# GpSimd's elementwise work in the long convolution runs on VectorE

## The chip, the cores and the metric

The kernel runs on one core of one Trainium2 chip. The metric is the device time of one execution, in microseconds (us); the median of three runs is 2259.96 (2259.07 to 2260.71). A core has TensorE (PE in the profile, PEld for its weight loads), VectorE (DVE), ScalarE (ACT), GpSimd (POOL) and SyncE (SP), which here issues most of the DMAs. Each engine executes its own queue in order and waits for the others by semaphores.

## The reference

One encoder layer on 512 tokens of width 2048: a projection, a gated mixer on one half of its columns, a Hyena operator on the other, an output projection, a gated feed-forward block, norms between them. The change is in the Hyena operator's convolution:

```python
u = bv * bx1
yc = bidir_long_conv(u, k).astype(x.dtype) + u * hy_d_skip[l]
y_b = bx0 * yc

def bidir_long_conv(v, k):
    L = v.shape[1]
    V = jnp.fft.rfft(v.astype(jnp.float32), n=2 * L, axis=1)
    K = jnp.fft.rfft(k, n=2 * L, axis=0)
    return jnp.fft.irfft(V * K[None], n=2 * L, axis=1)[:, :L]
```

## The kernel before

Matrices are multiplied to full fp32 accuracy as three products of fp32r pairs: `exact_pair` casts a tile to its high part on ScalarE (line 131) and subtracts it on VectorE for the low part (line 132); `mm3` issues high times high, low times high, high times low (lines 170 to 172). Weights stream in units of two K tiles by 512 columns: a DMA into `raw`, a cast `hi`, a difference `lo`, three buffers of each.

The stage of the change multiplies the first half of the output projection (`po`, 12 matmuls of 512 columns to a K tile) and works on the long convolution between its K tiles. The convolution goes in four chunks c = 0 to 3 of 256 channels, each in these steps:

- `turn`: 8 transposes on TensorE (`ut`) and the pair `uH`, `uL`.
- `forward`: 24 matmuls of 256 columns (`fw`), sums of cosines and sines.
- `products`: ScalarE copies two banks, VectorE takes sums and differences (lines 829, 830) and the butterfly (339 to 344) into `G`: two frequency halves i, each with a real and an imaginary part of 512 columns.
- `products2`: the complex product with the filter `kh`. For each half there are four multiplications, two on VectorE (840, 842) and two on GpSimd (841, 843), and then a difference and a sum on VectorE (847, 848).
- `spectra`, parity 0 and then 1: the sum, or the difference, of the halves, the real part on VectorE (856) and the imaginary part on GpSimd (857), and then the pair `sH`, `sL` of 1024 columns.
- `inverse`, parity 0 and 1: 24 matmuls (`iv`) each, which need `sH` first and `sL` for every third one.
- `finish`: for two tiles of 128 channels the skip term (880, 881), the product with x0 on GpSimd (882), the pair `ybH`, `ybL` (885, 886) and the running sum of squares `acc_b` (892 on ScalarE, 893 on GpSimd).

`go_to(n)` says behind how many K tiles of `po` a step is written. For chunk c the order on TensorE is: `fw`, six K tiles of `po` (72 matmuls), `iv` of parity 0, `ut` of the next chunk, one K tile, `iv` of parity 1, one K tile, and the next `fw`. The last chunk has no `ut`; its inverses stand among the first K tiles of the projection's second half (`po<-ybH`). A scheduler that builds the program may move an instruction a few places within a queue. Behind the stage, `mc` sums `acc_b` over the partitions.

Of the kernel before, what the change touches and what calls it, by code (L numbers as in the profile page):

```python
# [15 lines left out]
ALU = mybir.AluOpType  # L16

P = 128
# [12 lines left out]
CC = 256  # L31
# [11 lines left out]
def encoder_kernel(ctx: ExitStack, tc: tile.TileContext, a: dict, out: bass.AP):  # L43
# [16 lines left out]
    def bank(name):  # L60
        """one of the four banks of the streamed products"""
        return psum.tile([P, 512], F32, tag="mm", name=name, bufs=4)

    def sbank(name):
        """one of the four banks of everything that runs between them"""
        return psum.tile([P, 512], F32, tag="sd", name=name, bufs=4)
# [10 lines left out]
    # ---------------------------------------------------------------- the stream of weights  # L77
    # a unit: rows k0*128.. of a weight, nk K tiles by nc_ columns
# [25 lines left out]
    # beside the long convolution half of the low parts are computed on Pool  # L104
# [13 lines left out]
    def load_raw(key):  # L118
        src, k0, nk, c0, n = key
        raw = wp.tile([P, 2, 512], F32, tag="raw", name="raw", bufs=3)  # L120
        rows = src[k0 * P : (k0 + nk) * P, c0 : c0 + n].rearrange("(k p) c -> p k c", p=P)
        if st_["dma"] == 0:
            # the first one in halves, as the products wait for it
            for k in range(nk):
                SP.dma_start(raw[:, k : k + 1, :n], rows[:, k : k + 1, :])
        else:
            SP.dma_start(raw[:, :nk, :n], rows)
        return raw
# [27 lines left out]
    def next_unit(key):  # L156
        """the exact fp32r pair of the next unit; the two after it are already on their way"""
        i = st_["use"]
        assert plan[i][1:] == key[1:] and plan[i][0] is key[0], (i, key)
        split_to(i + 3)  # L160
        dma_to(i + 4)
        st_["use"] += 1
        return split_units.pop(i)
# [10 lines left out]
    # ---------------------------------------------------------------- x and constants  # L174
# [50 lines left out]
    def rsqrt(r, ss, n):  # L225
        """r = (ss / n + eps) ** -0.5"""
        DVE.tensor_scalar(r, ss, 1.0 / n, EPS, ALU.mult, ALU.add)
        POOL.tensor_tensor(r, r, nhalf.broadcast_to(list(r.shape)), ALU.pow)

    def rms_col(acc, n, name):  # L230
        """squares, to be summed over the partitions too -> 1/rms, [token, 1] per tile of tokens"""
        nt = acc.shape[-1] // P
        o = sbank("mc")
        for t in range(nt):
            PE.matmul(o[:, t : t + 1], acc[:, t * P : (t + 1) * P], ones[:, 0:1], start=True, stop=True)
        r = const.tile([P, NT], F32, tag="rc", name=name, bufs=3)
        rsqrt(r[:, :nt], o[:, :nt], n)
        return r

    def row_of(r, name, nt=NT):  # L240
        """[token, 1] columns -> the same row of tokens on all partitions"""
        o = sbank("mr")
        for t in range(nt):
            PE.matmul(o[:, t * P : (t + 1) * P], r[:, t : t + 1].broadcast_to([P, P]), ident, start=True, stop=True)
        row = const.tile([P, L], F32, tag="rb", name=name, bufs=2)
        ACT.copy(row[:, : nt * P], o[:, : nt * P])
        return row
# [23 lines left out]
    # ---------------------------------------------------------------- implicit filter  # L271
# [7 lines left out]
    # the last layer comes out twice, on both halves of the partitions  # L279
# [25 lines left out]
    # features of the lags: rows 0..63 the high parts, 64..127 the low parts  # L305
# [3 lines left out]
    def mlp_out():  # L309
        h = hcur[-1]  # L310
        t = fm.tile([P, L], F32R, name="h3t")
        ACT.copy(t, h)
        ACT.copy(h3[:FO, :], h[:FO, :])
        DVE.tensor_tensor(h3[FO:, :], h[FO:, :], f32(t[FO:, :]), ALU.subtract)
        # the backward half has no tap at lag 0
        DVE.tensor_copy(h0, f32(h3[:, :P]))
        DVE.tensor_scalar(h0[:, 0:1], f32(h0[:, 0:1]), 0.0, None, ALU.mult)
# [5 lines left out]
    def forward_mm(cs, tab, rH, rL):  # L323
        """cos (0) or sin (1) sums of the four token phases [tok, CC] -> banks [128, 2, CC] of phases 0 1, 2 3"""
        Hs, Ls = tab
        res = []
        for half in range(2):
            o = sbank("fw")
            ov = o.rearrange("p (m c) -> p m c", m=2)
            for m in range(2):  # L330
                r = 2 * half + m
                mm3(ov[:, m, :], Hs[:, r, cs, :], Ls[:, r, cs, :], rH[:, r, :], rL[:, r, :], True, True)
            res.append(o)
        return res

    def butterfly(G, U, T):
        """phase sums (U: 0+2, 1+3; T: 0-2, 1-3) [P, cs, 2, CC] -> frequencies f + 256 j:
        G[:, i, cs, m] holds j = 2 i + m"""
# [13 lines left out]
    def filter_pieces(tab):  # L352
# [31 lines left out]
        for c in range(NCC):  # L384
# [36 lines left out]
            # the sum of both directions goes with cos and their difference with sin;  # L421
            # the odd phases, which the frequencies f + 256 and f + 768 turn by a quarter, need both
# [47 lines left out]
    # ---------------------------------------------------------------- projections  # L470
    def projA(src, c0, nf, done, rhs=None):
        """[feature, token] tiles of h @ src[:, c0 : c0 + nf*128]; done(ps) takes them out of the banks"""
# [33 lines left out]
    # value branch, [token, feature]  # L506
# [22 lines left out]
    ug, x0 = [], []  # L529

    def eo(ap):
        """[P, 512] stored by token modulo 4, seen in token order"""
        return ap.rearrange("p (r m) -> p m r", r=4)
# [4 lines left out]
    # centred depthwise convolutions over tokens (free axis)  # L538
    def conv3(pl, ps, r, names, fb, to=None):
        """to: where the result goes, by token modulo 4; without it, in token order in a passing tile"""  # L540
# [48 lines left out]
    def go_to(n):  # L589
        """emit the products up to K tile n of the projections"""  # L590
        while pos[0] < n:
            next(main)
            pos[0] += 1

    # a_u, with the rest of x and the filter behind its K tiles
# [56 lines left out]
    # spatial gating weights, transposed: [j, h, i]  # L652
# [111 lines left out]
    # ---------------------------------------------------------------- long conv and output projection  # L764
# [42 lines left out]
    def turn(c):  # L807
        """[channel, token] -> [token, channel] pair of u"""
# [25 lines left out]
    def products2(c):  # L834
        (G, U, T), kh = conv[c].pop("G"), conv[c]["kh"]
        for i in range(2):
            vr, vi = flat(G[:, i, 0]), flat(G[:, i, 1])
            kr, ki = kh[:, i, 0, :], kh[:, i, 1, :]
            p1, p2 = flat(U[:, i]), flat(T[:, i])
            DVE.tensor_tensor(p1, vr, kr, ALU.mult)  # L840
            POOL.tensor_tensor(p2, vi, ki, ALU.mult)
            DVE.tensor_tensor(vr, vr, ki, ALU.mult)
            POOL.tensor_tensor(vi, vi, kr, ALU.mult)
        for i in range(2):
            vr, vi = flat(G[:, i, 0]), flat(G[:, i, 1])
            p1, p2 = flat(U[:, i]), flat(T[:, i])
            DVE.tensor_tensor(p1, p1, p2, ALU.subtract)
            DVE.tensor_tensor(vr, vr, vi, ALU.add)
        conv[c]["Y"] = (G, U, T)

    def spectra(c, par):
# [5 lines left out]
        POOL.tensor_tensor(flat(S[:, 1]), i0, i1, op)  # L857
# [17 lines left out]
    def finish(c):  # L875
        Dt, St = quad("T"), quad("U")
        for i in range(2):
# [4 lines left out]
            POOL.tensor_tensor(du, du, x0[ct], ALU.mult)  # L882
# [5 lines left out]
            if ct == 0:  # L888
                ACT.activation(pairs(acc_b), eo(du), AF.Square)
            else:  # L890
                sq = flat(St[:, i])
                ACT.activation(pairs(sq), eo(du), AF.Square)
                POOL.tensor_tensor(acc_b, acc_b, sq, ALU.add)
# [99 lines left out]
    # ---------------------------------------------------------------- ConvGLU  # L993
# [76 lines left out]
    # ---------------------------------------------------------------- the last group, and the final norm  # L1070
    # token halves, so that the first half leaves while the second is computed
# [36 lines left out]
    def rms3():  # L1108
        """1/rms per token from tiles of squares"""
# [17 lines left out]
    for th in range(2):  # L1127
        hs = slice(th * HW, (th + 1) * HW)
        # sums of squares: two running ones; at the end the last tiles go to the tensor engine as they are
# [42 lines left out]
def shape_constants():  # L1172
    """Tables that depend on the sequence length and widths alone."""
# [12 lines left out]
    # transforms of 1024 points at frequencies f + 1/2: forward [m, r, cos/sin, f] for token 4 m + r,  # L1186
    # inverse [f, parity e, cos/sin, kt, (q m)] for frequency f + 256 kt and token 4 m + 2 q + e
# [11 lines left out]
# the vectors that are used as per-partition columns, in one array  # L1199
# [20 lines left out]
def laid_out(inputs, zT):  # L1220
    """The inputs as the kernel reads them: the same numbers, some of them transposed or packed."""
# [31 lines left out]
```

## Time and profile before

| | |
|---|---|
| median of three runs | 2259.96 us (2259.07 to 2260.71) |
| span of the profiled execution | 2257.4 us |
| its own time beside the span | not printed; the runs' median is 2.6 us above the span |
| TensorE busy | 2189.7 us, 97% of the span |
| VectorE busy | 1133.1 us, 50% |
| ScalarE busy | 671.9 us, 30% |
| GpSimd busy | 317.5 us, 14% |
| the stage of the change | about 533 to 709 us of the span |

Busy shares are averages over the whole span. What ends a wait in the stage is read from the waits of TensorE and from the timeline.

### The profile page before, as it was taken

Reading aid. Unit: us, or ns where it says so; the run is one execution under the profiler, and the core shown is the slowest. Engines: PE = TensorE matmul, PEld = TensorE weight load, DVE = VectorE, ACT = ScalarE, POOL = GpSimd, SP = SyncE. Lnnn points to the kernel's source line nnn. Section 1 sums busy time; section 2 is a strip of 40 time slices with the busy share of each in tenths; the row PEclk is TensorE's granted clock in tenths of the full one; section 3 lists DMA queues with packets and bytes.
Section 4 is the critical chain, followed back from the end, with each engine's and each line's share of the span. In section 5 each row is a group of like instructions: output and inputs, shape, how many; then the busy total and the mean of one; then the engine's idle time right before and its main releaser. Section 6 shows DMA issues by size and latency. Waiting matters only on the chain.

```text
span 2257.4 us, 23811 instructions
## 1 busy us (share of the span) xinstructions
PE 2189.7 (97%) x9742; PEld 1782.5 (79%) x9742; DVE 1133.1 (50%) x1320; ACT 671.9 (30%) x851; POOL 317.5 (14%) x201
## 2 busy tenths in 40 slices
PE   7999999999888999999999999999999999999997
PEld 5778887778777888787887878878787887878877
DVE  8664465556676853534336353443534335343456
ACT  5333432222343332222122221222222122221333
POOL 5221121001344520101001010000101001010003
PEclk9999999999898999999999999999999999999998
DMA  6333223243212423222322323222222222222332
GB/s 208 99 109 122 85 87 92 83 131 111 86 66 93 140 93 96 93 92 94 102 95 93 94 92 95 91 96 94 94 92 95 93 94 93 93 94 85 95 120 75
DMA packets 113480, 223.10 MB, mean 99 GB/s; under 512 B 7035, under 2 KB 18491, under 8 KB 111580
## 3 DMA queue, kind: packets, MB, share of 16 engines
q1 hardware_dynamic: 109184, 215.69, 29.5%
q10 hardware_dynamic: 4188, 5.90, 0.8%
q8 instruction: 76, 1.25, 0.2%
q14 instruction: 32, 0.26, 0.0%
HBM read 213.18 MB, written 8.39 MB: 98 GB/s over the span
## 4 chain that ended last, share of the span: by engine, by line
PE 84%; DVE 10%; issue 2%; POOL 1%; DMA 1%; ACT 1%; SPq 0%; DVEq 0%; POOLq 0%; ACTq 0%
PE pa L170 19%; PE pa L172 19%; PE pa L171 19%; PE pd L170 5%; PE pd L172 5%; PE pd L171 5%; DVE cv L559 2%; DVE lo L132 1%; PE po L170 1%; PE po L171 1%; PE po L172 1%; PE pv L170 1%; PE pv L171 1%; PE pv L172 1%; DVE ev L546 1%
## 5 line engine op out<-in xcount | busy, mean ns | idle before, releaser
L132 DVE TENSOR_TENSOR lo<-raw,hi 128x1024 fp32r<-128x1024 f32 (+2 forms) x369 | 462.6, 1256 | 899.5 <-ACT hi L131 899.4
L131 ACT CAST hi<-raw 128x1024 fp32r<-128x1024 f32 (+2 forms) x369 | 382.3, 1036 | 1156.1 <-PE pa L171 738.2
L170 PE MATMUL pa<-h2H,hi 128*128 128x512 f32 x1376 | 543.6, 395 | 0.0
L172 PE MATMUL pa<-h2H,lo 128*128 128x512 f32 x1376 | 543.4, 395 | 0.0
L171 PE MATMUL pa<-h2L,hi 128*128 128x512 f32 x1376 | 543.4, 395 | 0.0
L172 PEld LDWEIGHTS pa<-h2H,lo 128*128 128x128 f32 x1376 | 258.4, 188 | 62.5
L170 PEld LDWEIGHTS pa<-h2H,hi 128*128 128x128 f32 x1376 | 258.4, 188 | 62.4
L171 PEld LDWEIGHTS pa<-h2L,hi 128*128 128x128 f32 x1376 | 258.4, 188 | 62.4
L170 PE MATMUL pd<-aH,hi 128*128 128x512 f32 x640 | 249.8, 390 | 14.8 <-DVE xacc L1048 14.8
L172 PE MATMUL pd<-aH,lo 128*128 128x512 f32 x640 | 249.2, 389 | 0.0
L171 PE MATMUL pd<-aL,hi 128*128 128x512 f32 x640 | 249.1, 389 | 0.0
L1011 POOL TENSOR_TENSOR gg<-gg,r 128x512 f32<-128x512 f32 x43 | 73.9, 1723 | 1243.8 <-ACT gg L1010 1243.8
L172 PE MATMUL pa<-hH,lo 128*128 128x512 f32 x512 | 206.2, 403 | 6.0 <-DVE lo L132 6.0
L170 PE MATMUL pa<-hH,hi 128*128 128x512 f32 x512 | 207.5, 405 | 1.2 <-DVE ev L546 1.2
L171 PE MATMUL pa<-hL,hi 128*128 128x512 f32 x512 | 205.8, 402 | 0.0
L170 PEld LDWEIGHTS pd<-aH,hi 128*128 128x128 f32 x640 | 120.1, 188 | 43.6 <-ACT hi L131 17.2
L172 PEld LDWEIGHTS pd<-aH,lo 128*128 128x128 f32 x640 | 120.1, 188 | 25.1
L171 PEld LDWEIGHTS pd<-aL,hi 128*128 128x128 f32 x640 | 120.1, 188 | 24.9
L1048 DVE TENSOR_TENSOR xacc<-xacc,pd 128x512 f32<-128x512 f32 x160 | 106.0, 685 | 42.4 <-PE pd L172 42.4
L172 PEld LDWEIGHTS pa<-hH,lo 128*128 128x128 f32 x512 | 98.7, 193 | 32.7 <-DVE lo L132 8.1
L170 PEld LDWEIGHTS pa<-hH,hi 128*128 128x128 f32 x512 | 99.0, 193 | 29.1 <-DVE ev L546 4.2
L171 PEld LDWEIGHTS pa<-hL,hi 128*128 128x128 f32 x512 | 98.6, 193 | 22.0
(243 smaller groups left out, 2305.1 us busy)
## 6 DMA issues: line engine op xcount, KB each, us to landing
raw<-in_ffn_w_up SPq DMA_DIRECT2D x160, 512.0 KB, 3.5
raw<-in_ffn_w_down SPq DMA_DIRECT2D x84, 512.0 KB, 3.5
raw<-in_w_in SPq DMA_DIRECT2D x79, 512.0 KB, 3.6
raw<-in_w_out SPq DMA_DIRECT2D x32, 512.0 KB, 3.5
raw<-in_ffn_w_up SPq DMA_DIRECT2D x16, 384.0 KB, 3.2
khat_d<-kh SPq DMA_DIRECT2D x4, 1024.0 KB, 3.9
kh<-khat_d SPq DMA_DIRECT2D x4, 1024.0 KB, 4.8
res<-in_xT SPq DMA_DIRECT2D x4, 1024.0 KB, 4.7
```

Source lines behind the costliest of these rows:

```text
L131: ACT.copy(hi, src)
L132: eng.tensor_tensor(lo, src, f32(hi), ALU.subtract)
L170: PE.matmul(o, ah, bh, start=start, stop=False)
L171: PE.matmul(o, ah, bl, start=False, stop=False)
L172: PE.matmul(o, al, bh, start=False, stop=stop)
L546: DVE.tensor_tensor(eo(e), pairs(o), pairs(r), ALU.mult)
L559: DVE.scalar_tensor_tensor(dd, e[:, from_ : from_ + z_ - a_], w(f), dd, ALU.mult, ALU.add)
L1011: POOL.tensor_tensor(g_, g_, r2[0], ALU.mult)
L1048: DVE.tensor_tensor(x_, x_, o, ALU.add)
```

## The change

Everything that GpSimd did in `products2`, `spectra` and `finish` is issued on VectorE. In `products2` each operation covers both frequency halves in one instruction of 2 x 512 columns. Comments and docstrings are gone too, so the lines behind have other numbers: line 857 of before is 855, 882 is 880, 886 is 884, 893 is 891.

```diff
     def products2(c):
         (G, U, T), kh = conv[c].pop("G"), conv[c]["kh"]
-        for i in range(2):
-            vr, vi = flat(G[:, i, 0]), flat(G[:, i, 1])
-            kr, ki = kh[:, i, 0, :], kh[:, i, 1, :]
-            p1, p2 = flat(U[:, i]), flat(T[:, i])
-            DVE.tensor_tensor(p1, vr, kr, ALU.mult)
-            POOL.tensor_tensor(p2, vi, ki, ALU.mult)
-            DVE.tensor_tensor(vr, vr, ki, ALU.mult)
-            POOL.tensor_tensor(vi, vi, kr, ALU.mult)
-        for i in range(2):
-            vr, vi = flat(G[:, i, 0]), flat(G[:, i, 1])
-            p1, p2 = flat(U[:, i]), flat(T[:, i])
-            DVE.tensor_tensor(p1, p1, p2, ALU.subtract)
-            DVE.tensor_tensor(vr, vr, vi, ALU.add)
+
+        Gv = G.rearrange("p i s m c -> p i s (m c)")
+        vr, vi = Gv[:, :, 0], Gv[:, :, 1]
+        kr, ki = kh[:, :, 0, :], kh[:, :, 1, :]
+        p1, p2 = (t.rearrange("p i m c -> p i (m c)") for t in (U, T))
+        DVE.tensor_tensor(p1, vr, kr, ALU.mult)
+        DVE.tensor_tensor(p2, vi, ki, ALU.mult)
+        DVE.tensor_tensor(vr, vr, ki, ALU.mult)
+        DVE.tensor_tensor(vi, vi, kr, ALU.mult)
+        DVE.tensor_tensor(p1, p1, p2, ALU.subtract)
+        DVE.tensor_tensor(vr, vr, vi, ALU.add)
         conv[c]["Y"] = (G, U, T)
...
         DVE.tensor_tensor(flat(S[:, 0]), r0, r1_, op)
-        POOL.tensor_tensor(flat(S[:, 1]), i0, i1, op)
+        DVE.tensor_tensor(flat(S[:, 1]), i0, i1, op)
...
-            POOL.tensor_tensor(du, du, x0[ct], ALU.mult)
+            DVE.tensor_tensor(du, du, x0[ct], ALU.mult)
...
-                POOL.tensor_tensor(acc_b, acc_b, sq, ALU.add)
+                DVE.tensor_tensor(acc_b, acc_b, sq, ALU.add)
```

First place: VectorE's queue of a chunk from the end of the butterfly to `sL` of parity 0. Before:

```order
L840 TENSOR_TENSOR U<-G,kh 128x512 x2
L842 TENSOR_TENSOR G<-G,kh 128x512 x2
L847 TENSOR_TENSOR U<-U,T 128x512
L848 TENSOR_TENSOR G<-G 128x512
L847 TENSOR_TENSOR U<-U,T 128x512
L848 TENSOR_TENSOR G<-G 128x512
L132 TENSOR_TENSOR lo<-raw,hi 128x1024
L856 TENSOR_TENSOR T<-U 128x512
L856 TENSOR_TENSOR U<-U 128x512
L132 TENSOR_TENSOR lo<-raw,hi 128x1024
L132 TENSOR_TENSOR sL<-T,sH 128x1024
```

The same stretch of the changed kernel:

```order
L841 TENSOR_TENSOR U<-G,kh 128x1024
L842 TENSOR_TENSOR T<-G,kh 128x1024
L843 TENSOR_TENSOR G<-G,kh 128x2x512
L844 TENSOR_TENSOR G<-G,kh 128x2x512
L845 TENSOR_TENSOR U<-U,T 128x1024
L846 TENSOR_TENSOR G<-G 128x2x512
L132 TENSOR_TENSOR lo<-raw,hi 128x1024
L854 TENSOR_TENSOR T<-U 128x512
L855 TENSOR_TENSOR T<-G 128x512
L132 TENSOR_TENSOR lo<-raw,hi 128x1024
L854 TENSOR_TENSOR U<-U 128x512
L132 TENSOR_TENSOR sL<-T,sH 128x1024
```

Eight instructions of 512 columns became six of 1024, the imaginary sum (855) stands among them, and the real difference of parity 1 (854, into U) now comes behind the second `lo`.

Second place: VectorE's queue in the `finish` of chunk 1, up to the first sum of chunk 2 (829); x is the tile x0. Of the changed kernel:

```order
L879 SCALAR_TENSOR_TENSOR T<-iv,rl_111,T 128x512
L880 TENSOR_TENSOR T<-T,x_3539 128x512
L879 SCALAR_TENSOR_TENSOR T<-iv,rl_111,T 128x512
L884 SCALAR_TENSOR_TENSOR ybL<-T,cols,ybH 128x512
L891 TENSOR_TENSOR acc_b<-acc_b,U 128x512
L880 TENSOR_TENSOR T<-T,x_3545 128x512
L132 TENSOR_TENSOR lo<-raw,hi 128x1024
L884 SCALAR_TENSOR_TENSOR ybL<-T,cols,ybH 128x512
L891 TENSOR_TENSOR acc_b<-acc_b,U 128x512
L829 TENSOR_TENSOR U<-fw,G 128x512
```

Before there stood 881 twice, 886 twice, `lo` and 829. The products with x0 (880) and the sums (891) now stand between them; in the `finish` of chunk 0 the one sum comes behind both 884 and the `lo` behind that.

Third place: TensorE's queue where the inverse of chunk 1 begins, as a piece of the difference:

```order
 L170 MATMUL iv<-invH,sH 128x2x128
 L171 MATMUL iv<-invL,sH 128x2x128
+L170 MATMUL iv<-invH,sH 128x2x128
+L171 MATMUL iv<-invL,sH 128x2x128
+L813 MATMUL ut<-ident,u 128x128 x4
 L172 MATMUL iv<-invH,sL 128x2x128
 L170 MATMUL iv<-invH,sH 128x2x128
```

Four matmuls with `sH` and four transposes stand before the first one with `sL` (172), where two matmuls stood. In chunk 0 three matmuls stand there, in chunk 2 four, eight transposes and one of `po`, in chunk 3 four and five of `po`.

## Rows read from the trace of the kernel before

**Rows 1.** The page: the span, and busy time, share and instructions of each engine.

```profile
span 2257.4 us, 23811 instructions
PE 2189.7 (97%) x9742; PEld 1782.5 (79%) x9742; DVE 1133.1 (50%) x1320; ACT 671.9 (30%) x851; POOL 317.5 (14%) x201
```

**Rows 2.** Waits of TensorE: who waited for whom, us in total, times, longest.

```profile
PE iv L170 <- ACT sH L131: 14.4, 4, 4.3
PE iv L172 <- DVE sL L132: 8.9, 4, 2.4
PE mc L235 <- POOL acc_b L893: 1.3, 1, 1.3
```

**Rows 3.** Timeline of TensorE in chunk 0: start, us, instructions [idle before <-releaser].

```profile
545.03 0.28 PE L170 MATMUL fw<-uH,tabH 128*128 128x256 f32 x1
...
566.10 0.39 PE L170 MATMUL iv<-invH,sH 128*128 128x256 f32 x1 [1.66 <-ACT sH L131]
...
569.03 0.39 PE L172 MATMUL iv<-invH,sL 128*128 128x256 f32 x1 [2.43 <-DVE sL L132]
...
573.25 1.05 PE L813 MATMUL ut<-ident,u 128*128 128x128 f32 x8
574.05 0.47 PE L170 MATMUL po<-yh,hi 128*128 128x512 f32 x1
...
579.79 0.40 PE L170 MATMUL po<-yh,hi 128*128 128x512 f32 x1
```

**Rows 4.** The same timeline in chunk 1.

```profile
582.55 0.28 PE L170 MATMUL fw<-uH,tabH 128*128 128x256 f32 x1
...
585.43 0.39 PE L170 MATMUL po<-yh,hi 128*128 128x512 f32 x1
...
606.13 0.58 PE L170 MATMUL iv<-invH,sH 128*128 128x256 f32 x1 [4.17 <-ACT sH L131]
...
609.06 0.58 PE L172 MATMUL iv<-invH,sL 128*128 128x256 f32 x1 [2.14 <-DVE sL L132]
...
620.59 0.40 PE L170 MATMUL po<-yh,hi 128*128 128x512 f32 x1
```

**Rows 5.** TensorE by windows: stretch, its length, busy, PEclk (granted clock), DMA.

```profile
610.00:613.00 3.00, 3.00 (x16) 0.50 0.00 0
```

**Rows 6.** Timeline of VectorE in chunk 1.

```profile
587.61 0.68 DVE L829 TENSOR_TENSOR U<-fw,G 128x512 f32<-128x512 f32 x1
...
592.55 1.28 DVE L840 TENSOR_TENSOR U<-G,kh 128x512 f32<-128x512 f32 x2
...
599.17 1.76 DVE L848 TENSOR_TENSOR G<-G 128x512 f32<-128x512 f32 x1 [1.18 <-POOL G L843]
...
605.59 1.22 DVE L132 TENSOR_TENSOR lo<-raw,hi 128x1024 fp32r<-128x1024 f32 x1
606.72 2.29 DVE L132 TENSOR_TENSOR sL<-T,sH 128x1024 fp32r<-128x1024 f32 x1
```

**Rows 7.** Timelines of GpSimd and of ScalarE in chunk 1.

```profile
597.40 2.99 POOL L843 TENSOR_TENSOR G<-G,kh 128x512 f32<-128x512 f32 x2
...
605.03 1.04 ACT L131 CAST sH<-T 128x1024 fp32r<-128x1024 f32 x1 [7.13 <-DVE T L856]
```

**Rows 8.** Instructions on G: ns min/median/max, first and last start, forms.

```profile
L840 DVE TENSOR_TENSOR U<-G,kh x8: 675/676/686, 552.5 to 674.9; 128x512 f32<-128x512 f32 x8
L841 POOL TENSOR_TENSOR T<-G,kh x8: 1282/2364/3486, 552.7 to 677.9; 128x512 f32<-128x512 f32 x8
```

**Rows 9.** The same view of T, the steps of `finish`.

```profile
L881 DVE SCALAR_TENSOR_TENSOR T<-iv,rl,T x8: 750/751/752, 578.6 to 701.8; 128x512 f32<-128x512 f32 x8
...
L885 ACT ACTIVATE ybH<-T,cols x8: 1214/1236/1237, 580.8 to 704.8; 128x512 fp32r<-128x512 f32 x8
L886 DVE SCALAR_TENSOR_TENSOR ybL<-T,cols,ybH x8: 1144/1158/1162, 582.1 to 706.0; 128x512 fp32r<-128x512 f32 x8
L892 ACT ACTIVATE U<-T x7: 1137/1138/1152, 584.1 to 705.9; 128x512 f32<-128x512 f32 x7
```

## The prediction

> **What bounds the kernel now.** I read the waits of TensorE first, since VectorE and GpSimd are busy for 50% and 14% of the span only [rows 1]. TensorE waits for little: 14.4 us for `sH` and 8.9 us for `sL`, four times each, once per chunk of the convolution, and 1.3 us for `acc_b` [rows 2]. Whatever the change does, it must do there. Next I read TensorE's timeline, to see what such a wait costs. In chunk 0 it idles 1.66 and 2.43 us [rows 3], in chunk 1 4.17 and 2.14 us [rows 4]; taking both from the 23.3 us of the two wait rows leaves 12.9 for chunks 2 and 3, so these are like chunk 1.
>
> The wait is not all of it. An undisturbed chunk, from its first `fw` to the `po` behind the second inverse, takes 2.88 for 24 matmuls of 256 columns, 585.43 to 601.96 (606.13 less the idle 4.17) for 72 of `po`, 16.4 without the last one's tail [rows 4], 2.88 for the first inverse (the shape of `fw`), 0.80 for the transposes [rows 3], a sixth of 16.4 for 12 more of `po`, and 2.88 for the second inverse: 28.6 us. Chunk 0 takes 34.8 [rows 3] and chunk 1 38.0 [rows 4], so they lose 6.2 and 9.4 us, 2.1 and 3.1 more than the idle time. [...] The stage loses 6.2 + 3 x 9.4 = 34.4 us, and 1.3 at `mc`. That is the most that can come back, apart from some clock behind `mc`.
>
> Last I read VectorE and GpSimd in chunk 1, to see why `sH` is late. From the start of 840 at 592.55 to `sH` at 605.03 there are 12.5 us [rows 6, 7]. GpSimd's products take 1.28 us at best but 2.36 in the median and 3.49 at most [rows 8]. The 848 that starts at 599.17 takes 1.76 and ends 0.54 us after GpSimd's last product (597.40 + 2.99 = 600.39) [rows 6, 7], while the shape alone takes 0.68 [rows 8]. So beside each other the two engines take turns, and one pays for the other's operation. The `sL` of 2.29 us beside a `lo` of the same size at 1.22 shows it once more [rows 6]. [...]
>
> **The change part by part.** I count from F, the first `fw` of a chunk. TensorE reaches the inverse at F + 19.3 (601.96 - 582.55, less the tail of a matmul) [rows 4].
>
> *products2.* Six VectorE instructions of 1024 columns replace eight of 512 and four of GpSimd. The nearest row is the low part of 1024 columns, which starts 1.13 us before the next instruction [rows 6]. Six make 6.8 us. The trace has no instruction of this form with two strided halves; I take the contiguous price. Three of the six touch neighbouring parts of G and may wait for the one ahead of them to end, 1.22 instead of 1.13 [rows 6] and some hundredths for the semaphore: 0 to 0.4 us, and I take 0.4, since they rewrite in place what their neighbours read. Chunk 1 begins them at 592.55 = F + 10.0 [rows 6] and ends at F + 17.2.
>
> *spectra, parity 0.* A `lo` (1.13), two sums of 512 (0.6 to the next, 840's two take 1.28 together [rows 6], and 0.68), then the cast of 1.04 [rows 7] and 0.1 for signals: `sH` at F + 20.75, against 606.07 - 582.55 = F + 23.5 now. Behind the sums VectorE does a `lo`, the real difference of parity 1 and then `sL`: 1.13 + 0.6 + 1.22, so `sL` is there at F + 22.5, against F + 26.5 now (609.06).
>
> *finish.* From X, the `po` behind the second inverse (579.79 in chunk 0), the steps alternate between VectorE and ScalarE: 881 ends at 579.3 [rows 9], the product with x0 is there at X + 0.25, `ybH` (1.24) at 1.5, `ybL` (1.16) at 2.7 [rows 9]. The second product with x0 is queued behind this `ybL`, which waits for ScalarE, and ends at 3.3; `ybH` 4.6, the square (1.14) 5.7, the sum (0.68) 6.4. The cast of `hi` is queued behind the square, and `lo` behind that: VectorE starts 829 at X + 7.8, where it starts now (587.61) [rows 6]. So chunk 1 gains nothing here. In the `finish` of chunks 1 and 2 the cast stands ahead of the second `ybH` and `lo` ahead of the second `ybL`, so the last sum ends at X + 7.0: chunks 2 and 3 begin 0.8 us earlier. The two products and one or two sums add 2.0 to 2.7 us to VectorE per chunk; they are hidden in its waits for ScalarE. If that cover were gone, 829 and with it `sH` would move by as much.
>
> *What TensorE then waits.* Chunk 0 has no `finish` ahead of it: 840 starts at 552.5 [rows 8] = F + 7.5 [rows 3], 2.5 us sooner than in chunk 1. `sH` is there at F + 18.25, no wait; `sL` at F + 20.0, three matmuls of 0.12 behind the start at 19.3: wait 0.35. Chunk 1: 1.45 for `sH`; four matmuls and four transposes cover 0.9, then 0.85 for `sL`: 2.3 us. Chunks 2 and 3, 0.8 earlier: 0.65, then a cover of 1.5 to 1.6, then 0.2: 0.85 each. Will the clock still fall? No row has a wait of 2.3 us spread over 3.2; the nearest, chunk 0 of before with 4.1 us, costs 2.1. I take 0 to 2.1 for chunk 1, 1.3 as the value, and 0 for the others.
>
> *mc.* The last sum ends at X + 7.0, and 28 matmuls of `po` (6.4 us) stand ahead of `mc` now: a wait of 0.65 for 1.3.
>
> **The sum.** 34.4 - (0.35 + 2.3 + 1.3 + 0.85 + 0.85) = 28.8, and 0.65 at `mc`: 29.4 us. The queues behind the stage keep their order, so nothing of it is given back. Span 2257.4 [rows 1] - 29.4 = 2228.0; the runs' median lies 2.6 above the span, which gives 2230.6 beside 2259.96 before.
>
> The two ends: every wait and all slow clock gone, with some clock behind `mc`, gives 37 us, 2223. With `sL` and `sH` a further 1.5 us late in each chunk, and the clock falling as in chunk 0, the remains are 1.9, 7, 4.5 and 4.5 us, 18 in all, which gives 2242.
>
> [...] The row has the next instruction start 1.13 us after one of 1.22 [rows 6], which is the price in the sum. [...]
>
> **The rivals.**
> - *The chain stays late.* Strided halves or waits between VectorE's own instructions make the six cost 1.4 us instead of 1.13, and the clock falls in three chunks: the upper end above, 2236 to 2246. For it speaks that the six rewrite G, U and T in place, one behind the other; against it, that two products of 512 that do the same start 0.60 apart now (840's pair takes 1.28) [rows 6]. 17%.
> - *The wait moves.* The stall ends, but VectorE's longer queue delays a `lo` or a `uL` on which `po` or `fw` waits, for some 4 us a chunk: 2246 to 2255. Against it: a `lo` is made two units, four K tiles or 11 us, ahead of its use, and the last one ahead of `iv` moves forward with the chain. 5%.
> - *Slower.* The long durations of 848 are VectorE's own price for these operands and not GpSimd's doing. Then an operation of 1024 columns costs 2 x 1.22, the mean of 1.76 and 0.68 [rows 6, 8], six take 14.6 us, `sH` comes at F + 28.6, 5.1 us later than now, and the stage pays some 18 to 20 us: 2279. It decides from 1.67 us an instruction, where the 3.3 us by which `sH` is early are used up. Against it: 840 reads the same tiles and takes 0.68 in all eight instances [rows 8]. 5%.
> - *No effect.* TensorE meets another wait at the same place, such as the bank of an inverse or the next weights, worth what it saved: 2256 to 2264. No row of TensorE's waits names one. 3%.
>
> **How the numbers follow.** The forecast has 70%, with 2223 to 2236 as its own range. The range 2223 to 2242 adds most of the first rival. A change of 0.2%, 4.5 us, is about what this measurement can tell. Faster: the forecast and the first two rivals, 92%; same 3%; slower 5%.
>
> **What the profile after should show.** TensorE's waits for `sH` and `sL` together at 3 to 7 us instead of 23.3, none for `sH` in chunk 0 and the longest in chunk 1; the six instructions at 1.13 to 1.25 us; no VectorE instruction of this stage above 1.3 us; 829 at X + 7.8 in chunk 1 and X + 7.0 in chunks 2 and 3; a granted clock of 1.0 in chunks 0, 2 and 3. I am wrong if one of the six takes over 1.4 us, if the clock falls in chunks with less than a microsecond of wait, or if a new wait stands under `fw` or `po`.

## The result, and the profile after

The changed kernel takes 2227.07 us in the median of four runs (2226.78 to 2228.73), the kernel before, run beside it, 2259.55 (2259.07 to 2260.71): 0.9857 times, with a 95% interval of 0.9843 to 0.9871. It is faster by 32.5 us. The forecast was 2230.6, in a range of 2223 to 2242.

The page of the changed kernel, the span and the busy time of each engine:

```profile
span 2225.5 us, 23765 instructions
PE 2179.2 (98%) x9742; PEld 1773.4 (80%) x9742; DVE 1134.9 (51%) x1335; ACT 672.4 (30%) x851; POOL 251.8 (11%) x162
```

The first thing to see is VectorE. GpSimd gave up 39 instructions and 65.7 us, VectorE took them all, and its own busy time rose by 1.8 us [rows 1]. By an estimate from the 0.60 to 0.68 us that an operation of 512 columns takes, the 39 would cost VectorE some 24 us. By the same estimate about 22 us of what the profile of before counted as VectorE's work was time in which it stood beside a GpSimd operation.

The waits of TensorE (who for whom, us in total, times, longest), to be held against [rows 2]:

```profile
PE iv L170 <- ACT sH L131: 1.7, 3, 1.0
...
PE iv L172 <- DVE sL L132: 0.6, 1, 0.6
PE mc L235 <- DVE acc_b L891: 0.6, 1, 0.6
```

23.3 us of waits for the spectra became 2.3, and no new one stands under `fw` or `po` in the stage. TensorE's timeline (start, us, instruction, idle time before it), for [rows 3] and [rows 4]:

```profile
545.56 0.28 PE L170 MATMUL fw<-uH,tabH 128*128 128x256 f32 x1
...
574.32 0.40 PE L170 MATMUL po<-yh,hi 128*128 128x512 f32 x1
...
577.08 0.28 PE L170 MATMUL fw<-uH,tabH 128*128 128x256 f32 x1
...
597.45 0.39 PE L170 MATMUL iv<-invH,sH 128*128 128x256 f32 x1 [0.97 <-ACT sH L131]
...
599.25 0.38 PE L172 MATMUL iv<-invH,sL 128*128 128x256 f32 x1 [0.61 <-DVE sL L132]
...
607.80 0.40 PE L170 MATMUL po<-yh,hi 128*128 128x512 f32 x1
...
678.44 1.05 PE L235 MATMUL mc<-ones,acc_b 128*128 128x1 f32 x8 [0.60 <-DVE acc_b L891]
```

Chunk 0, from its first `fw` to the `po` behind its second inverse, takes 574.32 - 545.56 = 28.8 us instead of 34.8, chunk 1 607.80 - 577.08 = 30.7 instead of 38.0; chunks 2 and 3, read in the same way, take 29.5 and 28.5 instead of 38.1 and 37.3. From the last of these `po` to the `mr` behind `mc` it is 12.7 us (671.29 to 684.00) instead of 15.0 (701.58 to 716.58). I call the sum of the five the stage time: 163.3 us before, 130.2 after, 33.1 less. The whole span is 31.9 less; the difference lies outside the stage (its first `fw` alone comes 0.5 us later than in [rows 3]).

TensorE by windows (stretch, length, busy, granted clock, DMA share, GB/s), for [rows 5]:

```profile
597.00:601.00 4.00, 2.94 (x22) 1.00 0.68 226
601.00:605.00 4.00, 4.00 (x25) 1.00 0.42 131
678.00:682.00 4.00, 3.56 (x20) 1.00 0.32 110
```

Before, the granted clock behind the waits was 0.60 in chunk 0 (569.03 to 573.00) and 0.50 in chunk 1 (606.13 to 614.00). By an estimate from TensorE's busy time there, 3.97 us at 0.60 and 5.73 at 0.50, that is 1.6 of the 2.1 us and 2.9 of the 3.1 us that these chunks lost beside their idle time. Now it is 1.00 in chunk 1 in and behind the two waits, and behind `mc` as well. The same view over the whole stage, from the first `fw` to `mr`, before and after:

```profile
545.03:716.58 171.55, 147.04 (x742) 0.89 0.24 83
```

```profile
545.56:684.00 138.44, 135.54 (x742) 1.00 0.31 103
```

VectorE and ScalarE in chunk 1, and the first sum of chunk 2, for [rows 6] and [rows 7]:

```profile
582.15 0.68 DVE L829 TENSOR_TENSOR U<-fw,G 128x512 f32<-128x512 f32 x1
...
587.08 1.22 DVE L841 TENSOR_TENSOR U<-G,kh 128x1024 f32<-128x1024 f32 x1
588.22 1.22 DVE L842 TENSOR_TENSOR T<-G,kh 128x1024 f32<-128x1024 f32 x1
589.35 1.22 DVE L843 TENSOR_TENSOR G<-G,kh 128x1024 f32<-128x1024 f32 x1
...
596.35 1.04 ACT L131 CAST sH<-T 128x1024 fp32r<-128x1024 f32 x1 [3.93 <-DVE T L855]
...
597.97 1.23 DVE L132 TENSOR_TENSOR sL<-T,sH 128x1024 fp32r<-128x1024 f32 x1
...
615.00 0.69 DVE L829 TENSOR_TENSOR U<-fw,G 128x512 f32<-128x512 f32 x1
```

The six take 1.22 us and start 1.13 to 1.14 apart. `sH` ends 10.3 us behind the start of the first (597.39 - 587.08); it was 13.5 behind 840 [rows 6, 7].

### The profile page after: what moved, and what is told of

It reads as the page before. It is cut to its first block, busy times and chain, and to the rows that moved or that the text cites. A ratio compares the mean times of both kernels' runs of the same rounds, so it can differ in the third digit from the quotient of the medians.

```text
span 2225.5 us, 23765 instructions
## 1 busy us (share of the span) xinstructions
PE 2179.2 (98%) x9742; PEld 1773.4 (80%) x9742; DVE 1134.9 (51%) x1335; ACT 672.4 (30%) x851; POOL 251.8 (11%) x162
## 4 chain that ended last, share of the span: by engine, by line
PE 87%; DVE 9%; issue 2%; DMA 1%; ACT 1%; SPq 0%; DVEq 0%; POOL 0%; ACTq 0%
PE pa L170 19%; PE pa L172 19%; PE pa L171 19%; PE pd L170 5%; PE pd L171 5%; PE pd L172 5%; DVE cv L559 2%; PE po L170 2%; PE po L171 2%; PE po L172 2%; PE pv L170 1%; PE pv L171 1%; PE pv L172 1%; DVE lo L132 1%; DVE ev L546 1%
## 5 line engine op out<-in xcount | busy, mean ns | idle before, releaser
L171 PEld LDWEIGHTS pa<-hL,hi 128*128 128x128 f32 x512 | 98.7, 193 | 22.1
```

Of the source, the lines that this page charges most:

```text
L171: PE.matmul(o, ah, bl, start=False, stop=False)
```

## Experiments

**The theories.** A: VectorE and GpSimd take turns, as I read the 1.76 us of 848 beside GpSimd's product for 0.68 without [rows 6, 8], so the way to `sH` and `sL` costs the sum of both, and GpSimd's operations are the dear ones (1.28 us at the least for VectorE's 0.68 [rows 8]); the gain is that they are gone from it. B: the gain comes from fewer and longer instructions, the merging over the halves. C: it comes from `finish`, by an earlier start of the next chunk and the earlier `mc`. The first three kernels are before with one part of the change each; the next five set A and B apart, take `finish` from the other side and look for what is left; the last two are a repeat.

**e1, products2 alone.** Before, with `products2` as in the change; `spectra` and `finish` stay.

```diff
-            DVE.tensor_tensor(p1, vr, kr, ALU.mult)
-            POOL.tensor_tensor(p2, vi, ki, ALU.mult)
...
+        DVE.tensor_tensor(p1, vr, kr, ALU.mult)
+        DVE.tensor_tensor(p2, vi, ki, ALU.mult)
```

> The kernel before with products2 alone as in the change; spectra and finish keep GpSimd. Theory A (VectorE and GpSimd take turns, so the time up to sH and sL is the sum of both, and what the change shortens is this chain): the products bring most, but GpSimd's imaginary sums still take turns with a lo and with sL, so sL comes about 1.4 us later than in the changed kernel; TensorE's waits for sH and sL at 7 to 11 us, 2233 to 2240. Theory B (the larger, fewer instructions are what counts): 2227 to 2230. Theory C (the finish, by which a chunk starts sooner, is what counts): over 2245.

Measured: 2243.09 us, 0.9937 (0.9924 to 0.9951); stage time 146.9, 16.4 less. That is less of a gain than the 2233 to 2240 expected. TensorE's waits:

```profile
PE iv L170 <- ACT sH L131: 10.5, 4, 3.3
...
PE iv L172 <- DVE sL L132: 3.0, 4, 0.8
```

The wait for `sH` is far from gone. Timelines of GpSimd and VectorE where the sums of chunk 1 stand:

```profile
595.31 4.42 POOL L855 TENSOR_TENSOR T<-G 128x512 f32<-128x512 f32 x1 [13.01 <-DVE G L846]
...
597.94 0.68 DVE L854 TENSOR_TENSOR U<-U 128x512 f32<-128x512 f32 x1
600.85 1.23 DVE L132 TENSOR_TENSOR sL<-T,sH 128x1024 fp32r<-128x1024 f32 x1 [2.23 <-ACT sH L131]
```

The one imaginary sum left on GpSimd takes 4.42 us, and the next of the same shape 1.26. It starts at 595.31, while VectorE has work without a gap until 598.62 (597.94 + 0.68), and ends 1.1 us after that. So it did not end behind the next VectorE instruction, as turns would have it, but at 599.73, with three VectorE instructions started in between and the run over, and VectorE then idled 2.23 us for the `sH` made from it. A's direction holds; I had priced the operation by its turns.

**e2, spectra alone.** Before, with `POOL.tensor_tensor(flat(S[:, 1]), i0, i1, op)` on DVE.

> The kernel before with only the imaginary sums of spectra on VectorE. Theory A: sH 0.4 and sL 1.5 us sooner in each chunk, waits for both at 15 to 19 us, 2248 to 2255. Theories B and C: 2258 to 2261, as before.

Measured: 2249.79 us, 0.9957 (0.9944 to 0.9969); stage time 154.1, 9.1 less, as A has it. TensorE's waits, its timeline in chunk 0 and the window behind it:

```profile
PE iv L170 <- ACT sH L131: 12.3, 4, 3.8
...
PE iv L172 <- DVE sL L132: 4.6, 4, 1.3
```

```profile
561.84 0.38 PE L170 MATMUL iv<-invH,sH 128*128 128x256 f32 x1 [1.11 <-ACT sH L131]
...
563.63 0.39 PE L172 MATMUL iv<-invH,sL 128*128 128x256 f32 x1 [1.29 <-DVE sL L132]
```

```profile
565.00:569.00 4.00, 4.00 (x24) 0.61 0.11 42
```

The wait for `sL` halves: the `sL` of parity 0, which took 2.29 us beside GpSimd's second sum, takes 1.21 without it (chunk 1); the wait for `sH`, behind the products, hardly moves. Chunk 0 idles 1.11 + 1.29 = 2.4 us, and the granted clock behind that is low here too (0.61 from 565 to 569). This case is taken up below.

**e3, finish alone.** Before, with the product with x0 and the sum into `acc_b` on DVE.

> The kernel before with only the finish (the product with x0 and the sum acc_b) on VectorE. Theory A: chunks 2 and 3 start 0.8 us sooner, the wait at mc halves and the clock behind it stays up: 3 to 4.5 us, 2255 to 2257. Theory C: half of the gain or more, 2244 or less. Theory B: 2260.

Measured: 2253.02 us, 0.9972 (0.9961 to 0.9982); stage time 155.4, 7.9 less, a little more of a gain than the 2255 to 2257 expected. TensorE's waits:

```profile
PE iv L170 <- ACT sH L131: 13.0, 4, 4.2
...
PE iv L172 <- DVE sL L132: 6.7, 4, 2.4
...
PE mc L235 <- DVE acc_b L893: 0.6, 1, 0.6
```

Of the 7.9, 2.3 are at `mc` (0.7 of wait, the rest the clock behind it: 0.55 from 709.40 to 713.00 before, 1.00 from 703.05 to 706.65 here). The waits for the spectra lose 3.6, all in chunks 2 and 3. These begin 0.7 us earlier, and in chunk 3 TensorE's first matmul with `sL` stands 1.74 us behind the first one with `sH` (684.52 to 686.26), where it stood 2.93 behind (687.93 to 690.86): about the 1.79 of e2's chunk 0 (561.84 to 563.63). C holds for a quarter of the gain and no more. The three parts alone give 16.4 + 9.1 + 7.9 = 33.4 us of stage time and together 33.1. But in each of the three profiles the clock behind `mc` stayed at 1.00, which is worth 1.6 us and can be won once (from the last `po` to `mr` it is 13.4 us in e1 and in e2, with the wait for `acc_b` as before). Counted once, the three give 30.2: nearly the whole, with 3 us that only the parts together bring. TensorE's order can account for these 3 us, by an estimate. In e1 two matmuls, 0.5 us, stand before the first one with `sL`, as before the change. In the changed kernel the scheduler put more work there (the third place in the change): 1.2 us in chunk 1 (597.45 to 599.25 - 0.61) and 1.8 in chunks 2 and 3. With 0.5 us there it would wait some 1.3 us for `sL` in each of the three chunks, 3 us more in all than it does. No run changes that order alone.

**e4, all on VectorE but in halves.** The changed kernel, with the twelve operations of 512 columns in the loops of before, all on DVE. Against the kernel before, `products2` differs in two lines:

```diff
-            POOL.tensor_tensor(p2, vi, ki, ALU.mult)
+            DVE.tensor_tensor(p2, vi, ki, ALU.mult)
...
-            POOL.tensor_tensor(vi, vi, kr, ALU.mult)
+            DVE.tensor_tensor(vi, vi, kr, ALU.mult)
```

> The changed kernel with products2 in two halves again, twelve instructions of 512 columns, all on VectorE. Theory A: twelve at 0.60 make 7.2 us for 6.8, sH 0.4 us later in each chunk: 2228 to 2230. Theory B: most of the gain is lost, over 2240.

Measured: 2225.44 us, 0.985 (0.9836 to 0.9863), below the 2228 to 2230 that A expected; stage time 130.4, that of the changed kernel. In the profiled execution what is lower lies ahead of the stage (see the last section). TensorE's waits:

```profile
PE iv L170 <- ACT sH L131: 2.5, 3, 1.4
...
PE iv L172 <- DVE sL L132: 0.2, 1, 0.2
```

Twelve starts 0.60 us apart take 7.2 us, six 1.13 apart 6.8; the 0.4 show as 0.8 more for `sH` in three chunks, of which 0.4 come back at `sL`.

**e5, merged but shared.** Before, merged over the halves, with p2 and `vi * kr` still on POOL.

```diff
+        DVE.tensor_tensor(p1, vr, kr, ALU.mult)
+        POOL.tensor_tensor(p2, vi, ki, ALU.mult)
+        DVE.tensor_tensor(vr, vr, ki, ALU.mult)
+        POOL.tensor_tensor(vi, vi, kr, ALU.mult)
```

> The kernel before with both halves in one instruction, but shared between VectorE and GpSimd as before. Theory A: GpSimd's two products of 1024 columns take about 2.4 us each and cannot run beside VectorE's, two at 1.13, one sum and one difference at 1.13 make some 9.3 us for 9.5: 2255 to 2262. Theory B: half of the gain or more, under 2245.

Measured: 2256.56 us, 0.9989 (0.998 to 0.9997); stage time 160.1, 3.2 less. Timelines of both engines in chunk 1:

```profile
593.15 3.16 POOL L842 TENSOR_TENSOR T<-G,kh 128x1024 f32<-128x1024 f32 x1 [6.25 <-DVE G L344]
596.40 3.27 POOL L844 TENSOR_TENSOR G<-G,kh 128x1024 f32<-128x1024 f32 x1
...
594.09 3.31 DVE L843 TENSOR_TENSOR G<-G,kh 128x1024 f32<-128x1024 f32 x1
597.32 3.42 DVE L845 TENSOR_TENSOR U<-U,T 128x1024 f32<-128x1024 f32 x1
```

Here it is VectorE that pays. Its instruction that starts while GpSimd's is under way lasts 3.31 us and ends 1.09 behind it (597.40 against 596.31); alone the shape takes 1.22. The next pair repeats it (600.74 against 599.67). With e4 this settles B: merging gives nothing measurable without GpSimd, and a tenth of a per cent with it.

**e6, finish back on GpSimd.** The changed kernel, with the two operations of e3 on POOL again.

> The changed kernel with the finish back on GpSimd. Theory A: chunks 2 and 3 start 0.8 us later, and the wait at mc is 1.3 us again with the clock falling behind it: 2230 to 2233. Theory C: over 2240.

Measured: 2231.48 us, 0.9882 (0.9866 to 0.9897); stage time 135.3, 5.1 more than the changed kernel. TensorE's waits, its timeline in chunk 1, and a window:

```profile
PE iv L172 <- DVE sL L132: 3.5, 3, 1.2
...
PE mc L235 <- POOL acc_b L891: 1.3, 1, 1.3
```

```profile
596.02 0.39 PE L170 MATMUL iv<-invH,sH 128*128 128x256 f32 x1 [1.04 <-ACT sH L131]
...
597.82 0.39 PE L172 MATMUL iv<-invH,sL 128*128 128x256 f32 x1 [1.17 <-DVE sL L132]
```

```profile
599.00:603.00 4.00, 4.00 (x30) 1.00 0.43 147
```

The time is the expected one, but only in part for the expected reason. 0.7 of the 5.1 us are at `mc`, where the wait came back and the clock was still 1.00 behind it (681 to 685); and `sH` comes 0.7 later in chunks 2 and 3, as expected. But 2.9 are more waiting for `sL`, which follows `sH` by 1.8 us as in the changed kernel. What differs is TensorE's order, which the scheduler set anew: three matmuls, 0.6 us (596.02 to 597.82 - 1.17), stand before the first one with `sL`, where the changed kernel has 1.2 to 1.8 us of work. So `finish` itself is worth some 2 us from this side, and the rest is the order. In chunk 1 the clock is 1.00 behind 1.04 + 1.17 = 2.2 us of idle time, in about the pattern of e2's chunk 0, where 0.61 followed 2.4 us.

**e7, GpSimd kept busy beside.** The changed kernel, and in each chunk four products of GpSimd of 512 columns on a tile of its own, released by a small VectorE operation when the butterfly is done. Nothing waits for them but the small operation of the next chunk.

```diff
...
+        DVE.tensor_scalar(beside[:, 0:1], G[:, 1, 1, 1, 0:1], 0.0, 1.0, ALU.mult, ALU.add)
+        for _ in range(4):
+            POOL.tensor_tensor(beside, beside, beside, ALU.mult)
```

> The changed kernel with four GpSimd products of 512 columns on a tile of their own, started when the butterfly ends; nothing waits for them but the next chunk's. Theory A: the two engines don't work at the same time; either VectorE's operations beside them last over 1.3 us, by up to 5 us in all, and the waits for sH and sL come back (up to 2258), or GpSimd's last far over 1.28 us while VectorE's run on (from 2227). Rival (the long durations of before were each engine's own price): VectorE's stay at 1.22 us apart 1.13 and GpSimd's at 1.28, beside each other, and 2227 to 2229.

Measured: 2227.43 us, 0.9861 (0.9848 to 0.9875): the time of the changed kernel. Timelines of both engines in chunk 1:

```profile
588.48 13.45 POOL L838 TENSOR_TENSOR beside<-beside 128x512 f32<-128x512 f32 x1 [16.60 <-DVE beside L836]
...
588.32 1.21 DVE L848 TENSOR_TENSOR T<-G,kh 128x1024 f32<-128x1024 f32 x1
589.46 1.21 DVE L849 TENSOR_TENSOR G<-G,kh 128x1024 f32<-128x1024 f32 x1
...
601.02 1.99 DVE L132 TENSOR_TENSOR sL<-U,sH 128x1024 fp32r<-128x1024 f32 x1
```

GpSimd's first product lasts 13.45 us, until 601.93, and the five of VectorE's six that stand beside it take 1.21 each, for 1.22 in the changed kernel. At 601.02 a VectorE instruction for once starts no earlier than the one before it ends: the `sL` of parity 1. GpSimd's first product ends 0.91 us behind that start, and this `sL` takes 1.99 us instead of 1.23. TensorE's waits for the spectra are 1.9 and 0.5 us, as in the changed kernel.

**e8, spectra of parity 0 written earlier.** The changed kernel, with `spectra(c, 0)` ahead of `go_to(n + 8)`, straight behind the six, to remove the `lo` between them.

```diff
-            go_to(n + 8)
             spectra(c, 0)
+            go_to(n + 8)
```

> The changed kernel with the spectra of parity 0 written straight behind products2, so that the lo ahead of its sums comes behind them: sH 1.1 and sL 0.6 us sooner in each chunk. If the waits for sH and sL that are left (2.3 us) come from that place in VectorE's queue, they fall to 0.5 to 1.5 us: 2225 to 2227. If what is left lies elsewhere, 2227 and no change.

Measured: 2228.01 us, 0.9863 (0.985 to 0.9877): no gain. TensorE's wait for `sH` is gone, and one for `sL` of 2.8 us in three chunks (the longest 1.7) stands in its place. In chunk 1, VectorE's `sL` and TensorE's first matmul with it:

```profile
596.96 1.21 DVE L132 TENSOR_TENSOR sL<-T,sH 128x1024 fp32r<-128x1024 f32 x1
```

```profile
598.23 0.39 PE L172 MATMUL iv<-invH,sL 128*128 128x256 f32 x1 [1.70 <-DVE sL L132]
```

`sL` ends at F + 21.5 (F is 576.67), 0.6 sooner than in the changed kernel, as expected. But the order of TensorE changed once more: three matmuls, 0.6 us, stand before the first one with `sL`, where there were 1.2 us of work. What was won at `sL` is lost in that cover.

**The repeat: the changed kernel and e4's on one chip.**

> The changed kernel unaltered, beside the version in halves on the same chip. 2226 to 2229 by either reading.

> The same program as e4_halves. If one instruction over both halves is worth nothing that can be measured, it comes within 2 us of c1_changed, and e4_halves' lower time came from ahead of the stage. If twelve instructions of 512 columns are really better, it is 2 us or more below c1_changed again.

Measured: the changed kernel 2228.08 us (2224.46 to 2228.28), 0.9855 (0.9838 to 0.9871); in halves 2226.59 (2222.71 to 2227.67), 0.985 (0.9836 to 0.9865). The intervals nearly coincide: merged or in halves is the same. No run beat the changed kernel by 2 us; in the stage 2.9 us of waits are left.

## Why the prediction was right, step by step

- *What bounds the kernel* held: the gain came at the two waits and the clock behind them (0.60 and 0.50 before in chunks 0 and 1, 1.00 now). The 34.4 us said to be lost against undisturbed chunks come to 34.7 when all four chunks are read: 148.3 of chunk time against 3 x 28.6 + 27.8. Chunk 3 has no transposes (0.80 us), which the prediction had counted in it too.
- *products2.* 1.13 us apiece is what they take. The 0.4 us for waiting on each other, taken at the upper end of 0 to 0.4, was not paid: three of the six touch neighbouring parts of G and start no later than the others, 1.13 to 1.14 us behind the one ahead. So `sH` in chunk 1 came at F + 20.3 (597.39 - 577.08) for F + 20.75, `sL` at F + 22.1 for F + 22.5. An instruction of 1.22 us is followed by the next after 1.13, though the six work in place on G, U and T.
- *What TensorE waits.* 4.35 us forecast, 2.3 measured: chunk 0 nothing for 0.35, chunk 1 1.58 for 2.3, chunks 2 and 3 0.35 and 0.36 for 0.85 each. That is for the most part the 0.4 us once more. The rest is the cover ahead of `sL`, 1.2 us in chunk 1 and 1.8 in chunks 2 and 3, for the 0.9 and 1.5 to 1.6 taken.
- *finish.* 829 was to start at X + 7.8 in chunk 1 and X + 7.0 in chunk 2: it starts at 582.15 - 574.32 = X + 7.83 and 615.00 - 607.80 = X + 7.20. The operations added to VectorE lie under its waits for ScalarE, as said, and e3 and e6 confirm that they are better there, by some 2 us of e6's 5.1.
- *The clock in chunk 1* was mis-sized: the 1.3 us, taken from 0 to 2.1, were an estimate from chunk 0 of before that no run shows; in their place the runs showed a granted clock of 1.00 from 597 to 605 and so no loss. e2 and e6 lie on either side of it: 0.61 behind 2.4 us of idle time, 1.00 behind 2.2.
- *mc.* 0.60 us of wait for 0.65. But the clock behind it, which the sum left out and the range's lower end named, came back too (1.00 from 678 to 682): the way from the last `po` of the stage to the `mr` behind `mc` is 2.3 us shorter, the wait 0.7. That is 1.6 us more than forecast, and as the last section shows, not a sure gain.
- *The sum.* 28.8 + 2.05 of waits + 1.3 of clock is 32.1 for the chunks, 30.8 measured: 0.3 more was there to lose, and some 1.6 us remain beside the 2.3 of waits, at a granted clock of 1.00, which the sum had put at nothing; what they are is open. With 2.3 at `mc`, it is 33.1 for 29.4. At the upper end of the range the prediction's 7 us for chunk 1 don't follow from its own terms (2.3 + 1.5 + 2.1 = 5.9), and its 18 us would give 2243; nothing measured depends on it.
- *The mechanism*, "the two engines take turns, and one pays for the other's operation": the second half is what the runs bear out, in both directions (VectorE pays in e5, 3.31 us for 1.22, and in [rows 6], 1.76 for 0.68; GpSimd in e1, 4.42 for 1.26, and in e7, 13.45 where its shortest takes 1.04). That they alternate is not: in e7 a dozen VectorE instructions start while that one product of GpSimd lasts and take their usual 0.68 and 1.21 us, up to 601.02. Which of the two pays is open, see the last section.
- *The rivals.* The six at 1.4 us, the wait moved under `po` or `fw`, the long durations as VectorE's own price, and no effect: the rows after show none of them. e5 answers the third by itself, the same operand shapes at 3.3 us with GpSimd beside and 1.22 without.

## What to carry to other kernels

Where two operations of VectorE and GpSimd overlap in the trace and either lasts far beyond its shortest instance, count their sum and not the longer of them (in e5, 3.31 us for an operation of 1.22, of which 2.22 ran beside GpSimd's): on a chain that TensorE waits for, the work was better on VectorE here, although VectorE is the busier engine. Read an engine's busy time with that in mind, since part of it can be time beside the other engine (by the estimate above some 22 of VectorE's 1133 us). And price a short wait of TensorE with the clock behind it: of the 33.1 us, 21.7 were waiting (21.0 for the spectra, 0.7 at `mc`); the other 11.4 are mainly the stretches in and behind the waits at the lower clock; over the whole stage the granted clock was 0.89 before and is 1.00 now. Last, see what stands between the first work that needs `sH` and the first that needs `sL`: when a scheduler moves it, as in e6 and e8, a variant's time shows the new order too and not its own part alone.

## What the runs showed of the hardware that was not expected

Which one pays. The imaginary sum of parity 0 stands at the same place in e1 and in e5: released by the last of the six, it starts inside the `lo` behind it, and the real sum is VectorE's next. Its durations (ns, min/median/max of the four chunks) in e1, then in e5:

```profile
L855 POOL TENSOR_TENSOR T<-G x4: 4424/4450/4486, 559.4 to 670.0; 128x512 f32<-128x512 f32 x4
```

```profile
L855 POOL TENSOR_TENSOR T<-G x4: 2175/2177/2203, 562.4 to 682.0; 128x512 f32<-128x512 f32 x4
```

In chunk 1 of e5 it ends 1.12 us behind the end of that `lo` (604.13 against 603.01), and the real sum takes 1.75 us for 0.68; in e1 it ends 1.1 us behind the whole run of VectorE. Its durations are alike in all four chunks each time. In e5, VectorE's instructions had lasted 3.31 and 3.42 us beside GpSimd's products shortly before, in e1 1.22; whether that decides it no run shows, and the explanation above does not rest on it.

The granted clock. Idle times of 1.04 and 1.17 us, 1.8 apart, left it at 1.00 (e6); 1.11 and 1.29, as far apart, were followed by 0.61 (e2). At `mc` the same wait of 1.3 us was followed by different clocks. The windows behind it in the kernel before and in e6:

```profile
709.40:713.00 3.60, 3.60 (x11) 0.55 0.43 148
```

```profile
681.00:685.00 4.00, 3.85 (x21) 1.00 0.37 118
```

e5 is like the kernel before (0.58 from 707.3 to 711.0), e1 and e2 are like e6 (1.00). So behind a wait of 1.3 us the clock was low in two profiles of five; behind the 0.5 to 0.7 us that are left when `finish` is on VectorE (the changed kernel twice, e3, the halves twice, e7, e8) it stayed at 1.00 in all seven. Why it was low in those two only is open, and so the 1.6 us at `mc` belong to the change less surely than the rest.

The clock also varies between profiles of like kernels, far from the change. From 100 to 200 us it was 0.95 in the changed kernel and 0.98 in e4, whose code up to there is the same. e4's first `fw` of the stage starts 3.8 us earlier for it (541.78 against 545.56), so two spans of single profiles can differ by as much; the stage times above do not contain it.
